# Mixture-of-experts layer: two experts in one float32 tile, experts sorted on chip, wider weight units

## The chip, the cores and the metric

The program runs on one core of a Trainium2 chip, in one launch. The metric is the device time of one execution in microseconds (us), lower is better; each figure for a kernel is the median of several executions. One further execution was recorded by the profiler, and every row shown below is from that one.

## The reference, cut to what matters

Two layers of a diffusion transformer work on 256 latent tokens (and, in the first layer, 256 context tokens) of width 1024. Everything up to the last stage is the same in both kernels. The last stage is a mixture of experts on the 256 latent tokens:

```python
logits = (t @ router)                          # [256, 8]
top_val, top_idx = lax.top_k(logits, 2)
gates = sum(one_hot(top_idx, 8) * softmax(top_val)[..., None], axis=1)
for e in range(8):
    he = silu(t @ w_gate[e]) * (t @ w_up[e])   # 1024 -> 3584
    out = out + gates[:, e:e+1] * (he @ w_down[e])   # 3584 -> 1024
```

All arrays are float32. An expert has three matrices of 1024 x 3584 (14.7 MB each), all eight 352 MB. Each token goes to two experts, so the experts get 64 tokens on average. For the inputs that the reference draws with its default seed the eight counts are 36, 68, 77, 79, 34, 67, 89 and 62.

## The kernel before, in words

An expert's tokens are gathered into 128 slots by a product with a selection matrix; the result is kept transposed (feature by slot) as the stationary operand of TensorE, and the weights stream through as the moving operand, 512 columns at a time. To keep float32 accuracy at the rate of the rounded type float32r, every operand is held in two parts, high and low, and each product is three matmuls (`mm3`: high x high, low x high, high x low). The tokens are split once; the weights are split as they come: ScalarE (ACT) writes the high part `wh`, VectorE (DVE) the low part `wl`, each 1024 columns at a time.

Weights come in units of 1 MB ([128, 2048] float32). All are loaded by the queue of SyncE (SP), in program order, into a ring of places: four named `w`, two `x1w`, two `mw`, two `zw`, that is ten; in the first round five more places that later hold something else are used as well (`gw`, two `yw`, two `sp`). A place is free again when VectorE has made the low part from it. A unit of the gate or up matrix is four blocks of 128 rows by 512 columns (2 KB runs in memory), one of the down matrix two blocks by 1024 columns (4 KB runs).

The eight experts go one after another, each in seven chunks of 512 hidden units. `up_chunk` does the gate and the up product of a chunk (4 units), then silu, product and transposition; `down_chunk` adds the chunk before it into two PSUM banks (2 units). So an expert takes 42 units and 504 matmuls of 512 columns, plus 28 transpositions. After an expert `finish` evacuates the result and `scatter` puts it back on token rows. The engines run in the order that a scheduler chose at build time; each engine and each queue is strictly in order.

If an expert has more than 128 tokens a slow second round runs (`overflow_expert`, behind a branch at the end); with the counts above it does not.

Of the kernel before, what the change touches and what calls it, by code (L numbers as in the profile page):

```python
# [28 lines left out]
def build(tc, A, out, stages=("s0", "mix0", "ffn0", "mix1", "moe"), dbg=None):  # L29
# [57 lines left out]
    # ---------------------------------------------------------------- constants  # L87
# [8 lines left out]
    # conditions and parameter rows -> columns  # L96
# [34 lines left out]
    # token tiles: 0, 1 = ctx; 2, 3 = x  # L131
# [48 lines left out]
    def sqrt_table(after):  # L180
        """the table of the square root, ahead of its use, once the column after is there"""
# [7 lines left out]
    def rsqrt_(ss, n, inv_n, name, bias=None):  # L189
        """1 / sqrt(ss * inv_n + bias), [P, n]: the square root of ScalarE and a Newton step; bias: eps"""  # L190
# [11 lines left out]
    # ---------------------------------------------------------------- ada  # L202
# [60 lines left out]
    # pre-norm of the residual and modulation, transposed and split  # L263
# [41 lines left out]
    def prenorm_all(mod, h2, tp, perm=False):  # L305
        """from the residual in DRAM"""
# [6 lines left out]
    def boundary(t, x_, b2, rowg, mod, h2, tp, perm=False, store=None):  # L313
        """end of a branch and start of the next for one token tile"""
# [7 lines left out]
    def token_major(hH, hL, W, c0, cb_=None, gets=None):  # L322
        """[128 tokens, 512 columns] products of the four token tiles"""
# [12 lines left out]
    # residual stream in DRAM between its uses (token tiles: 0, 1 = ctx; 2, 3 = x)  # L336
# [14 lines left out]
    def postnorm(x_, b2, rowg, tp, ss=None, tmt=None, out_=None, eng=None):  # L351
        """x_ += rowg * rms_norm(b2), b2: two [P, 512] PSUM banks or SBUF halves; ss: sums of squares so far"""
# [3 lines left out]
        for h in range(2):  # L356
            if ss[h] is None:
                ss[h] = sumsq(b2[h], tp, *(("mdL", 2) if out_ else ()))
# [19 lines left out]
    # S5 operands in DRAM: E [(j, k'), g, (re | im, d, n)], F [(d, n), g, (re | -im, i, k)],  # L378
    # T [(j, k'), i, g, k], powers A [(d, n), level, (re re | -im im) by (g, part)]
# [11 lines left out]
    def reduce_angle(a, n):  # L391
        """a -> a - 2 pi round(a / 2 pi), in place; n: scratch"""
# [6 lines left out]
    def s5_prep():  # L399
        with tc.tile_pool(name="s5c", bufs=1) as pc_, ExitStack() as es5:  # L400
            # powers for E and F: re, im, re + im
# [112 lines left out]
            for g8 in range(8):  # L514
# [7 lines left out]
                # C: re, im, re + im, re - im; B: re, im, re + im, im - re  # L522
# [71 lines left out]
            # lag 0: both directions and the skip  # L594
# [15 lines left out]
    # hidden units of the SwiGLU, [unit, tile, token]  # L610
# [17 lines left out]
    def ffn_first(h2, tp, tag):  # L628
        """the first two tiles of hidden units: the contexts first, while the latents are being normed"""
# [15 lines left out]
    # =============================================================== layer 0 mixer  # L645
    later.append(ada_pair(1, 0))
    if "mix0" in stages:
        es0, es1, esB = ExitStack(), ExitStack(), ExitStack()
        open_ps(esB, "psB", 6)
        if True:  # L650
            mk = open_pool(es0, "mk")
            # ---- filters; norm of the tokens
# [40 lines left out]
            # the filter network on both halves of the partitions alike  # L693
# [16 lines left out]
            # high parts over low parts along the contraction  # L710
# [26 lines left out]
            def filter_spec():  # L737
                """spectra of the filters"""
# [52 lines left out]
            # k, v, q, token-major; q / k norm and rope; q^T, k^T  # L791
# [118 lines left out]
            # ---- hyena long convolutions and attention  # L910
# [7 lines left out]
            def conv_spec(src, o):  # L918
                """spectral product of the [P, 2, 512] token-major src with filter o"""
# [40 lines left out]
            def attn(s, h):  # L960
                """head h (kv head h // 4) of stream s: transposed weights [key, key tile, query]"""
# [58 lines left out]
        # =========================================================== layer 0: out projection  # L1020
# [35 lines left out]
    # =============================================================== layer 0: SwiGLU  # L1056
# [109 lines left out]
    def route_setup(mp, tp, hf):  # L1166
        """tables of the dispatch"""
# [5 lines left out]
        R_["tie"] = tp.tile([P, NE, NE], F32, name="tie")  # L1173
# [28 lines left out]
        # rank (ties: the lower index first): the two first are taken  # L1202
# [18 lines left out]
    def route_rows(t, x_):  # L1221
        """normed rows of a token tile, split"""
# [6 lines left out]
    def route_slots(tp, e2):  # L1229
        """slots of two experts: [token, (expert, slot)]"""  # L1230
        Sel = tp.tile([P, 2, 2, P], F32R, tag="Sel", name="Sel", bufs=1)
        for t in range(2):
            for e in range(2):
                V.tensor_scalar(Sel[:, t, e, :], iota, R_["posm"][:, t, e2 * 2 + e:e2 * 2 + e + 1], None, OP.is_equal)
        return Sel

    def route_gates(tp, m2):
# [3 lines left out]
        v = [m2.tile([P, 2, 1], F32, tag="md%s" % "HL"[i], name="v%d" % i) for i in range(2)]  # L1241
# [13 lines left out]
        b = bank("cnt", "x")  # L1255
# [4 lines left out]
    def route_scatter(tp, Sel):  # L1260
        """the slots of two experts, transposed"""
        SelT = tp.tile([P, 2, 256], F32R, tag="SelT", name="SelT", bufs=1)
        b = bank("selT", "x")
# [5 lines left out]
        return SelT  # L1269

    def modulate(dst, src, k, vec):
        """one k tile of gathered normed tokens, modulated"""
# [10 lines left out]
    def moe_space():  # L1283
        """room on chip for the weights of the experts, as it comes free"""
        x1 = hp.tile([P, 2, 2048], F32, tag="hL", name="x1w")
        mw = moep.tile([P, 2, 2048], F32, name="mw")
        more_raw(x1[:, 0], x1[:, 1], mw[:, 0], mw[:, 1])

    def moe_first(sp, w0=()):
        """units of the first chunk ahead of the dispatch; the first round uses tiles needed later, too"""  # L1290
# [5 lines left out]
        ws = [kload(A["od_moe_w_gate"][0, 0], 4 * u, 0, 512) for u in range(2)]  # L1296

        def split():
            for u in range(2):
                first[0, u] = wsplit(ws[u], eng=G)  # L1300
        return split

    # =============================================================== layer 1 mixer
# [604 lines left out]
```

## Time and profile before

| | us |
|---|---|
| median of 3 runs (lowest, highest) | 2045.88 (2043.07, 2050.94) |
| profiled execution: span from first to last instruction | 2044.3 |
| of it from the first expert matmul to the last one | 1048.3 to 2027 |

The profiled execution has no time of its own beside its span; its span lies 1.6 us under the median. In the table of slices a digit is the busy share of a 51 us slice in tenths. `PEclk` in a window is the granted TensorE clock as a share of full speed (1.00 is 2.4 GHz, 0.50 is 1.2 GHz). DMA is the mean busy share of the core's 16 DMA engines; it can pass 1 because a packet's time overlaps the next one's.

### The profile page before, as it was taken

How to read it: one execution, taken by the hardware profiler on the slowest of the kernel's cores; microseconds unless marked ns; L12 is line 12 of the kernel's file. 1: busy time of each engine (PE TensorE's matmuls, PEld its weight loads, DVE VectorE, ACT ScalarE, POOL GpSimd, SP SyncE). 2: the span in 40 equal slices, each digit the busy share in tenths (PEclk: the TensorE clock that was granted, in tenths of full speed). 3: DMA queues.
4: the chain of work that ended last, by engine and by line, in shares of the span. 5: the costliest groups of instructions: out<-in, count | busy, mean ns of one | idle time of the engine just before them, and what ended most of it. 6: DMA issues, size and time to landing. Idle time of an engine off the chain costs nothing. (4 is left out here: it accounts for less than half of the span.)

```text
span 2044.3 us, 26454 instructions
## 1 busy us (share of the span) xinstructions
PE 1913.2 (94%) x9648; PEld 1502.6 (74%) x9648; DVE 1605.5 (79%) x2224; ACT 1210.1 (59%) x1679; POOL 160.6 (8%) x143
## 2 busy tenths in 40 slices
PE   5999999989999998965879999999999999999997
PEld 2667667867777786754768888888888888788885
DVE  6575775688775476487689999998899898998987
ACT  3532355543332365423668778777777777777775
POOL 1000310001011001045310000000000000000000
PEclk9999999999999999977979999999999999999998
DMA  9474315437657557627777999999999999999992
GB/s 342 163 253 154 131 42 177 157 108 229 209 196 230 206 202 264 228 82 267 280 265 277 384 354 345 339 367 378 344 352 357 368 369 338 342 383 366 361 373 94
DMA packets 246123, 545.59 MB, mean 267 GB/s; under 512 B 32619, under 2 KB 62420, under 8 KB 238436
## 3 DMA queue, kind: packets, MB, share of 16 engines
q1 hardware_dynamic: 215036, 514.73, 69.7%
q10 hardware_dynamic: 29400, 23.50, 3.9%
q0 software_dynamic: 1552, 5.62, 1.0%
q8 instruction: 78, 1.28, 0.3%
q14 instruction: 57, 0.47, 0.1%
HBM read 517.85 MB, written 25.89 MB: 266 GB/s over the span
## 5 line engine op out<-in xcount | busy, mean ns | idle before, releaser
L187 DVE TENSOR_TENSOR wl<-w,wh 128x1024 fp32r<-128x1024 f32 x396 | 471.5, 1225 | 103.6 <-ACT wh L186 97.3
L186 ACT ACTIVATE wh<-w 128x1024 fp32r<-128x1024 f32 x406 | 410.5, 1054 | 159.9 <-PE gu L178 52.4
L177 PE MATMUL yb<-wh,mdL 128*128 128x512 f32 x448 | 179.9, 402 | 0.0
L178 PE MATMUL mgu<-wl,xgH 128*128 128x512 f32 x448 | 176.1, 393 | 0.3
L176 PE MATMUL yb<-wh,mdH 128*128 128x512 f32 x448 | 176.3, 394 | 0.0
L178 PE MATMUL mgu<-wl,xB 128*128 128x512 f32 x448 | 175.7, 392 | 0.3
L177 PE MATMUL mgu<-wh,xgL 128*128 128x512 f32 x448 | 175.9, 393 | 0.0
L176 PE MATMUL mgu<-wh,xgH 128*128 128x512 f32 x448 | 175.9, 393 | 0.0
L177 PE MATMUL mgu<-wh,xB 128*128 128x512 f32 x448 | 174.9, 390 | 0.0
L176 PE MATMUL mgu<-wh,xB 128*128 128x512 f32 x448 | 174.6, 390 | 0.0
L187 DVE TENSOR_TENSOR wl<-zw,wh 128x1024 fp32r<-128x1024 f32 x132 | 155.5, 1219 | 15.0 <-ACT wh L186 13.0
L187 DVE TENSOR_TENSOR wl<-x1w,wh 128x1024 fp32r<-128x1024 f32 x132 | 156.4, 1219 | 11.8 <-ACT wh L186 9.1
L187 DVE TENSOR_TENSOR wl<-mw,wh 128x1024 fp32r<-128x1024 f32 x132 | 156.1, 1219 | 10.9 <-ACT wh L186 8.3
L178 PE MATMUL yb<-wl,mdH 128*128 128x512 f32 x448 | 151.4, 393 | 0.0
L176 PE MATMUL gu<-hH,wh 128*128 128x512 f32 (+1 forms) x384 | 145.9, 380 | 2.2 <-ACT hH L186 2.2
L178 PE MATMUL gu<-hL,wh 128*128 128x512 f32 (+1 forms) x384 | 144.3, 377 | 0.0
L177 PE MATMUL gu<-hH,wl 128*128 128x512 f32 (+1 forms) x384 | 143.4, 374 | 0.0
L186 ACT ACTIVATE wh<-x1w 128x1024 fp32r<-128x1024 f32 x134 | 135.6, 1054 | 11.2 <-PE mgu L177 7.3
L186 ACT ACTIVATE wh<-mw 128x1024 fp32r<-128x1024 f32 x132 | 133.8, 1054 | 11.2 <-PE mgu L177 7.6
L186 ACT ACTIVATE wh<-zw 128x1024 fp32r<-128x1024 f32 x132 | 133.2, 1053 | 10.0 <-PE mgu L177 5.9
L178 PEld LDWEIGHTS mgu<-wl,xB 128*128 128x128 f32 x448 | 84.0, 188 | 23.3 <-DVE wl L187 2.7
L178 PEld LDWEIGHTS mgu<-wl,xgH 128*128 128x128 f32 x448 | 84.2, 188 | 21.6 <-DVE wl L187 2.1
(668 smaller groups left out, 3845.3 us busy)
## 6 DMA issues: line engine op xcount, KB each, us to landing
w<-in_ada_w_dram SPq DMA_DIRECT2D x48, 1024.0 KB
w<-in_od_moe_w_up_dram SPq DMA_DIRECT2D x45, 1024.0 KB
w<-in_od_moe_w_down_dram SPq DMA_DIRECT2D x44, 1024.0 KB
w<-in_od_moe_w_gate_dram SPq DMA_DIRECT2D x43, 1024.0 KB
mw<-in_od_moe_w_gate_dram SPq DMA_DIRECT2D x23, 1024.0 KB
zw<-in_od_moe_w_up_dram SPq DMA_DIRECT2D x23, 1024.0 KB
x1w<-in_od_moe_w_down_dram SPq DMA_DIRECT2D x23, 1024.0 KB
w<-in_ev_ffn_w_down_dram SPq DMA_DIRECT2D x22, 1024.0 KB
```

The costliest lines, as they stand in the source:

```text
L176: T.matmul(b, aH, bH, start=start, stop=False)
L177: T.matmul(b, aL, bH, start=False, stop=False)
L178: T.matmul(b, aH, bL, start=False, stop=stop)
L186: S.activation(h, src, AF.Copy)
L187: (eng or V).tensor_tensor(l, src, h.bitcast(F32), op=OP.subtract)
```

## The change

- Experts 0 and 1 stay as they are. Experts 2 to 7 are sorted by their token count on chip (`route_order`): six register values then say which expert stands at which place, and the loads of places 2 to 7 take the expert's number from a register (`eload`).
- The four places 2 to 5 with the larger counts are done as before, with three matmuls per product. The last two places (the two smallest counts) share one tile: 64 slots each, one in the left half and one in the right half of TensorE's columns. Their products are plain float32 matmuls on the unsplit weights (`up_pair`, `down_pair`): one matmul per expert in place of three, two experts side by side.
- Chunks are 1024 hidden units wide (the fourth of an expert is 512), and a unit of gate or up weights is two row blocks by 1024 columns. In `up_big` the two column halves of a unit are done one after the other, each over both row blocks.
- The four chunks of the pair are put between those of the six other experts, at places 2, 8, 14 and 20 of the list of 28 tasks.
- The ring has eight places: the two `mw` are gone (their room goes to the pair's tiles). `mdH` and `mdL` have one buffer of twice the width in place of two.
- The second round starts at 64 tokens for the two experts of the pair, at 128 for the others.

The core of the diff (new functions whole, the rest cut):

```diff
+    def eload(W, e, k0, c0, n):
+
+        if isinstance(e, int):
+            return kload(W[e], k0, c0, n)
+        nk = 2048 // n
+        w = raw_tile()
+        SY.dma_start(w.rearrange("p (k c) -> p k c", k=nk),
+                     W[bass.ds(e, 1), k0 * P:(k0 + nk) * P, c0:c0 + n].rearrange("o (k p) c -> p (o k) c", p=P))
+        return w
...
+        return [nc.values_load(numi[0:1, i:i + 1], engines=[mybir.EngineType.SP], min_val=0, max_val=NE - 1)
+                for i in range(n)]
...
-        mw = moep.tile([P, 2, 2048], F32, name="mw")
-        more_raw(x1[:, 0], x1[:, 1], mw[:, 0], mw[:, 1])
+        more_raw(x1[:, 0], x1[:, 1])
...
+            def up_big(s, c, xH, xL, so):
+                o, w = piece(c)
+                nh, nk = w // 512, 2048 // w
                 bs = []
                 for i, W in enumerate((Wg, Wu)):
...
+                    bb = [bank("mgu", "gu", 4) for _ in range(nh)]
+                    for u in range(KD // nk):
+                        get = first.pop((s, c, i, u), None) or wsplit(eload(W, num[s], nk * u, o, w))
+                        for h in range(nh):
+                            for kk in range(nk):
+                                k = nk * u + kk
+                                mm3(bb[h], xH[:, k, so:so + P], xL[:, k, so:so + P],
+                                    *get(kk * w + h * 512, 512), k == 0, k == KD - 1)
+                    bs.append(bb)
+                return hidden(bs)
+
+            def up_pair(c, xP):
+                o, w = piece(c)
+                nh, nk = w // 512, 2048 // w
+                bs = []
+                for W in (Wg, Wu):
+                    bb = [bank("pgu", "gu", 4) for _ in range(nh)]
+                    for u in range(KD // nk):
+                        ws = [eload(W, num[PAIR + i], nk * u, o, w) for i in range(2)]
+                        for kk in range(nk):
+                            k = nk * u + kk
+                            for h in range(nh):
+                                for i in range(2):
+                                    r = slice(64 * i, 64 * i + 64)
+                                    T.matmul(bb[h][r], xP[:, k, r], ws[i][:, kk * w + h * 512:kk * w + h * 512 + 512],
+                                             start=(k == 0), stop=(k == KD - 1))
+                    bs.append(bb)
+                return hidden(bs)
...
+            def down_pair(c, hT, yP):
+                o, w = piece(c)
+                bb = [bank("py", "gu", 4) for _ in range(2)]
+                for u in range(w // 256):
+                    ws = [eload(Wd, num[PAIR + i], o // P + 2 * u, 0, 1024) for i in range(2)]
+                    for f2 in range(2):
+                        f = 2 * u + f2
+                        for h in range(2):
+                            for i in range(2):
+                                T.matmul(bb[h][64 * i:64 * i + 64], hT[:, f * P + 64 * i:f * P + 64 * i + 64],
+                                         ws[i][:, f2 * 1024 + h * 512:f2 * 1024 + (h + 1) * 512],
+                                         start=(f == 0), stop=(f == w // P - 1))
...
+            PAIR = NE - 2
+            num = [0, 1]
...
+            tasks = [(s, c) for s in range(PAIR) for c in range(NP)]
+            for c, i in zip(range(NP), (2, 8, 14, 20)):
+                tasks.insert(i, (PAIR, c))
```

On the queue of SyncE, 20 units into the experts (the chunks of experts 0 and 1 that come first), before: the queue goes on with the next loads of the ring, whose addresses are known.

```order
L153 DMA w<-in_od_moe_w_down_dram 128x2x1024 x2
L153 DMA w<-in_od_moe_w_gate_dram 128x4x512
L153 DMA zw<-in_od_moe_w_gate_dram 128x4x512
L153 DMA zw<-in_od_moe_w_up_dram 128x4x512
L153 DMA x1w<-in_od_moe_w_up_dram 128x4x512
```

The same place after the change; `onumi` holds the six expert numbers, and the lines shown are the last of six reads of it and the first loads of the pair.

```order
L1316 TENSOR_LOAD onumi
L1316 ISA x2
L163 ISA
L163 DMA zw<-in_od_moe_w_gate_dram 128x2x1024
L163 ISA
L163 DMA x1w<-in_od_moe_w_gate_dram 128x2x1024
L163 ISA
```

Six reads of the table now stand in the queue, and each load whose expert comes from a register has one more instruction ahead of it.

On TensorE, a piece of one expert's gate product before (`mgu` is the PSUM bank, `wh` and `wl` the split weights, `xgH` and `xgL` the split tokens): three matmuls for each block of weights.

```order
L176 MATMUL mgu_9088<-wh_9090,xgH_8799 128x512
L177 MATMUL mgu_9088<-wh_9090,xgL_8800 128x512
L178 MATMUL mgu_9088<-wl_9091,xgH_8799 128x512
L176 MATMUL mgu_9088<-wh_9094,xgH_8799 128x512
L177 MATMUL mgu_9088<-wh_9094,xgL_8800 128x512
```

Where the pair's first chunk begins after the change (`pgu` are its two banks, `xP` the tokens of both experts; `zw` and `x1w` are here the units of its two experts):

```order
L188 MATMUL yb_8869<-wl_9476,mdH_9034 128x512
L1857 MATMUL mht_9493<-cpk_76,hd_9398 128x128 x4
L1844 MATMUL pgu_9509<-zw_8607,xP_9172 64x512
L1844 MATMUL pgu_9509<-x1w_8441,xP_9172 64x512
L1844 MATMUL pgu_9510<-zw_8607,xP_9172 64x512
L1857 MATMUL mht_9500<-cpk_76,hd_9401 128x128 x4
L1844 MATMUL pgu_9510<-x1w_8441,xP_9172 64x512
```

The pair's matmuls read the units as they were loaded; the two experts alternate, each into its own 64 partitions of a bank, and TensorE now waits for the load itself and not for a split.

## Rows read from the trace of the kernel before

**Rows 1.** The page: span, busy time, and 40 slices of the span.
```profile
span 2044.3 us, 26454 instructions
PE 1913.2 (94%) x9648; PEld 1502.6 (74%) x9648; DVE 1605.5 (79%) x2224; ACT 1210.1 (59%) x1679; POOL 160.6 (8%) x143
...
DVE  6575775688775476487689999998899898998987
...
DMA  9474315437657557627777999999999999999992
```
**Rows 2.** Windows over the expert stage: from:to, us, busy per engine (instructions), PEclk, DMA, GB/s.
```profile
1048.00:2027.00 979.00, 978.35 (x4433) 799.28 (x4431) 891.61 (x877) 747.36 (x832) 1.82 (x1) 1.00 0.95 345
1100.00:2000.00 900.00, 899.35 (x4072) 734.84 (x4071) 820.24 (x794) 685.33 (x762) 0.00 (x0) 1.00 0.99 360
```
**Rows 3.** Waits, 1100 to 2000: us in total, times, longest.
```profile
PEld mgu L178 <- DVE wl L187: 4.8, 12, 0.6
```
**Rows 4.** Waits of SyncE's queue, 1100 to 2000.
```profile
SPq L153 <- DVE wl L187: 751.4, 304, 7.3
```
**Rows 5.** Timeline of PE in mid-stage: start us, us, what; the first and last of eleven.
```profile
1499.73 0.40 PE L176 MATMUL mgu<-wh,xB 128*128 128x512 f32 x1
...
1502.02 0.39 PE L177 MATMUL mgu<-wh,xB 128*128 128x512 f32 x1
```
**Rows 6.** Groups by form, 1100 to 2000: busy us, mean ns, idle before.
```profile
L187 DVE TENSOR_TENSOR wl<-w,wh 128x1024 fp32r<-128x1024 f32 x248 | 291.9, 1219 | 24.7 <-ACT wh L186 20.8
L186 ACT ACTIVATE wh<-w 128x1024 fp32r<-128x1024 f32 x248 | 248.2, 1053 | 19.5 <-PE mgu L177 11.2 <-PE yb L177 5.5 <-PE mgu L178 1.5
L1727 DVE TENSOR_TENSOR hd<-mgu,hd 128x512 f32<-128x512 f32 x52 | 35.9, 690 | 18.9 <-PE mgu L178 18.9
L1730 PE MATMUL mht<-cpk,hd 128*128 128x128 f32 x204 | 30.8, 273 | 0.0
```
**Rows 7.** Timeline of PE in layer 0, two stretches with unsplit float32 matmuls.
```profile
265.10 1.88 PE L969 MATMUL sc<-kz,qT 128*128 128x512 f32 x4
...
105.14 1.07 PE L227 MATMUL adp<-w,scol 128*32 128x512 f32 x8
106.14 0.50 PE L176 MATMUL tm<-wh,hH 128*128 128x512 f32 x1
```
**Rows 8.** Timeline of SyncE's queue: the first expert loads, those around 1050, the last.
```profile
993.88 0.50 SPq L153 DMA_DIRECT2D gw<-in_od_moe_w_gate_dram  x1
...
1042.51 0.46 SPq L153 DMA_DIRECT2D x1w<-in_od_moe_w_down_dram  x1
1054.35 0.37 SPq L153 DMA_DIRECT2D x1w<-in_od_moe_w_gate_dram  x1
```
**Rows 9.** Windows with the DMA engines full, columns as in rows 2.
```profile
10.00:20.00 10.00, 4.24 (x16) 1.10 (x19) 5.58 (x14) 2.42 (x3) 2.04 (x4) 1.00 1.02 414
1004.00:1014.00 10.00, 10.00 (x45) 8.27 (x45) 7.10 (x11) 7.17 (x12) 0.63 (x1) 1.00 1.05 398
1125.00:1150.00 25.00, 25.00 (x112) 20.31 (x111) 22.83 (x22) 19.52 (x22) 0.00 (x0) 1.00 1.04 391
1175.00:1200.00 25.00, 25.00 (x113) 20.18 (x112) 24.17 (x26) 19.19 (x21) 0.00 (x0) 1.00 0.87 314
```
**Rows 10.** Timeline of PE: first and last expert matmuls.
```profile
1048.32 0.40 PE L176 MATMUL mgu<-wh,xgH 128*128 128x512 f32 x1
...
2026.57 0.62 PE L178 MATMUL yb<-wl,mdH 128*128 128x512 f32 x2
```
**Rows 11.** The line that reads a register from the chip's memory: min/median/max ns.
```profile
L1805 SPq TENSOR_LOAD <-mxi x1: 485/485/485, 1997.9 to 1997.9; - x1
L1805 SPq FUSED_REGOPS  x1: 177/177/177, 1998.4 to 1998.4; - x1
```
**Rows 12.** Windows where PE was short of work, columns as in rows 2.
```profile
885.00:895.00 10.00, 5.67 (x33) 4.47 (x31) 9.52 (x29) 2.33 (x5) 4.75 (x4) 0.94 0.51 168
895.00:915.00 20.00, 7.47 (x38) 7.47 (x38) 15.49 (x28) 5.55 (x12) 4.01 (x2) 0.52 0.06 21
```

More of the change, by code (lines that the diff above doesn't have):

```diff
@@ L1295, in moe_first @@
         r += [lambda: z[:, 0], lambda: z[:, 1]]
-        ws = [kload(A["od_moe_w_gate"][0, 0], 4 * u, 0, 512) for u in range(2)]
+        ws = [kload(A["od_moe_w_gate"][0, 0], 2 * u, 0, 1024) for u in range(2)]
         def split():
             for u in range(2):
-                first[0, u] = wsplit(ws[u], eng=G)
+                first[0, 0, 0, u] = wsplit(ws[u], eng=G)
         return split
@@ new lines, in build, with piece, hidden @@
+            NP = 4
+            def piece(c):
+                return c * 1024, min(1024, FFE - c * 1024)
+            def hidden(bs):
+                hds_ = []
+                for g, u in zip(*bs):
+                    hd = hd_tile()
+                    S.activation(hd, g, AF.Silu)
+                    V.tensor_tensor(hd, u, hd, op=OP.mult)
+                    hds_.append(hd)
+                return hds_
+            def up_big(s, c, xH, xL, so):
+                o, w = piece(c)
+                nh, nk = w // 512, 2048 // w
@@ new lines, in turn @@
+            def turn(hds_, pair):
+                n = 512 * len(hds_)
+                dH = m2.tile([P, 1024], F32 if pair else F32R, tag="mdH", name="hTP" if pair else "mdH", bufs=1)
+                dL = None if pair else m2.tile([P, 1024], F32R, tag="mdL", name="mdL", bufs=1)
+                for j, hd in enumerate(hds_):
+                    b = bank("mht", "mt", 1)
+                    for f in range(4):
+                        T.transpose(b[:, f * P:(f + 1) * P], hd[:, f * P:(f + 1) * P], ident)
+                    cs = slice(j * 512, (j + 1) * 512)
+                    if pair:
+                        S.activation(dH[:, cs], b, AF.Copy)
+                    else:
+                        split_to(dH[:, cs], dL[:, cs], b)
@@ L1749, in scatter @@
+            def scatter(acc, s, yH, yL):
                 for t in range(2):
+                    sT = SelT[PAIR][:, t * P:(t + 1) * P] if s == PAIR else SelT[s // 2][:, s % 2, t * P:(t + 1) * P]
                     for h in range(2):
-                        b = bank("sct", "gu" if t and e == NE - 1 else "x")
+                        b = bank("sct", "gu", 4) if t and s == PAIR - 1 else fbank("sct")
                         cs = slice(h * 512, (h + 1) * 512)
-                        T.matmul(b, SelT[e // 2][:, e % 2, t * P:(t + 1) * P], yH[:, cs], start=True, stop=False)
@@ L1754, in scatter @@
-                        T.matmul(b, SelT[e // 2][:, e % 2, t * P:(t + 1) * P], yL[:, cs], start=False, stop=True)
-                        V.scalar_tensor_tensor(acc[:, t, cs], b, gate[:, t, e:e + 1], acc[:, t, cs],
-                                               OP.mult, OP.add)
-            def finish(e, yb):
+                        T.matmul(b, sT, yH[:, cs], start=True, stop=False)
+                        T.matmul(b, sT, yL[:, cs], start=False, stop=True)
+                        if s == PAIR:
+                            V.tensor_tensor(acc[:, t, cs], b, acc[:, t, cs], op=OP.add)
+                        else:
+                            V.scalar_tensor_tensor(acc[:, t, cs], b, gate_of(t, s), acc[:, t, cs], OP.mult, OP.add)
@@ new lines, in build @@
+            for c, i in zip(range(NP), (2, 8, 14, 20)):
+                tasks.insert(i, (PAIR, c))
+            tasks.append(None)
+            pend, done, yP = None, [], None
+            for i, task in enumerate(tasks):
+                hd_ = None
+                if task is not None:
+                    s, c = task
+                    if s == PAIR:
+                        hd_ = up_pair(c, xP)
+                    else:
+                        if c == 0:
+                            ybs[s] = [bank("yb", "yb") for _ in range(2)]
+                        hd_ = up_big(s, c, *xs_[s // 2], (s % 2) * P)
+                for d in done:
+                    scatter(acc, *d)
+                done = []
+                if pend is not None:
+                    (s1, c1), d1 = pend
+                    if s1 == PAIR:
+                        if c1 == 0:
+                            yP = m2.tile([P, D], F32, name="yP", bufs=1)
+                        down_pair(c1, d1[0], yP)
+                        if c1 == NP - 1:
+                            done.append(finish(PAIR, yP))
+                    else:
+                        down_big(s1, c1, *d1, ybs[s1])
+                        if c1 == NP - 1:
+                            done.append(finish(s1, ybs.pop(s1)))
+                pend = (task, turn(hd_, s == PAIR)) if task is not None else None
+                if i == 0:
@@ new lines, in build @@
+            mxo = mp.tile([1, NE], F32, name="mxo")
+            mxc = mp.tile([1, 1], F32, name="mxc")
+            mxi = mp.tile([1, 1], I32, name="mxi")
+            V.tensor_tensor(mxo, cnt[0:1, :], R_["cap"][0:1, :], op=OP.subtract)
+            V.tensor_reduce(mxc, mxo, axis=AX.X, op=OP.max)
+            V.tensor_scalar(mxc, mxc, 0.0, None, OP.max)
+            V.tensor_copy(mxi, mxc)
+            rv = nc.values_load(mxi[0:1, 0:1], min_val=0, max_val=2 * P)
+            dP = [tc.dram_tile([NE, P, 4], F32, name="dP%d" % r) for r in range(2)]
@@ L1809, in build @@
+            with tc.tile_pool(name="ovf", bufs=1) as op_:
+                with tc.If(rv > 0):
+                    for r in range(2):
                         pk = hq.tile([P, NE, 4], F32, tag="hL", name="pk")
[L1810 removed]
+                        V.tensor_tensor(pk[:, :, 0:2], posm.rearrange("p t e -> p e t"),
+                                        R_["cap"].unsqueeze(2).to_broadcast([P, NE, 2]), op=OP.subtract)
+                        if r:
+                            V.tensor_scalar(pk[:, :, 0:2], pk[:, :, 0:2], float(-P), None, OP.add)
```

203 lines of the change are left out of this document (118 added, 85 removed).

## The prediction

> **What bounds the kernel now.** I first read the page: TensorE (PE) is busy for 94% of the span, and in the second half VectorE and the DMA engines stand near full too [rows 1]. So three resources may be the limit, and the expert stage has to be read by itself. Over its 979 us PE is busy for 978.35 us at the full clock [rows 2]. Then the waits: from 1100 to 2000 the longest wait of PE's weight loads, for a low part from VectorE, comes to 4.8 us in all [rows 3], while SyncE's queue waits 751 us for VectorE to free a place [rows 4]. The loads wait for the engines, not the engines for the loads. And matmuls of 512 columns start every 0.229 us (ten intervals in 2.29 us) [rows 5]: 4032 of them are 923 of the 979 us, and transpositions, gathers and scatters fill the rest. The stage is bound by PE, with VectorE at 820 of 900 us and DMA at share 0.99 and 360 GB/s close behind [rows 2]. What the change saves on PE therefore counts only until the next limit.
>
> **What it takes from PE.** Two experts lose 2 x 504 matmuls, 231 us. For them come 168 sets (112 gate and up, 56 down) of two float32 matmuls, one per expert. Nothing in the trace has two column groups of 64, so I take the price from both sides. Four unsplit float32 matmuls with 512 columns on the whole array take 1.88 us with the drain of the last, some 0.43 each [rows 7]. Eight in four column groups of 32 run from 105.14 to 106.14, so four side by side cost 0.5 us with the drain shared [rows 7]. A set is 0.44 us if its halves run side by side and 0.87 us if not; the group row is the nearer, so 0.44: 74 us in all, 146 at the other end. The Trainium skill (FP8 and Floating Point Precision, TensorE Precision Notes) says that true float32 takes four passes through the array. By that page a set would be four times 0.229, 0.92 us, and the pair 154 us. The row shows about two times 0.229, so I go by the row. With the pair's own gather (32 small products, about 4 us) PE alone would need 979 - 231 + 74 + 4 = 826 us: a saving of 153 us, and a kernel at 1891, if PE stayed the limit.
>
> **What the queue can give.** It can't stay so. All 336 units of 1 MB still have to come, and 336 MB x 1.0486 in 826 us would be 427 GB/s. Stretches with the DMA engines full give 398 GB/s with 2 KB runs, 391 with both kinds of run while all engines are busy, and 414 with 8 KB runs in the first layer [rows 9]. Where the share is lower (0.87) the rate is too (314) [rows 9]: there the loads had no place to go. After the change gate and up come in 4 KB runs, except in the fourth chunks (32 units). I take 400 GB/s for 4 KB, 2.62 us a unit, and 391, 2.68 us, for those 32; the ends are 414 (2.53 us) and 380 (2.76 us; the 360 of the stage at share 0.99, brought to share 1.04). The Trainium skill (DMA: Bandwidth & Descriptors, Where 436 GB/s comes from) says that about 358 GB/s per core is what memory gives. That is the stage's own mean, and by it a unit would take 2.93 us. The 398 and 414 of rows 9 speak against that as a ceiling.
>
> **The sum.** PE starts the experts at 1048.3 [rows 10]. Two chunks of 1024 and one down product come ahead of the pair: 20 units of 12 matmuls, 55 us, with transpositions and the pair's gather some 5 us, small waits 3 us: 1112. The first loads go out from 994 as before; the queue then stands still for want of places until about 1054 [rows 8], which the change does not alter (13 first places instead of 15). At 1112 the 20 units have been used and the ring of eight is full, so 28 have landed and 308 are to come.
>
> From there the queue is the limit, because the pair's chunk eats its units faster than they come: two units (5.2 us) feed four sets (1.8 us). A whole chunk of the pair is 24 units, 63 us of loads, for 21 us of PE. In the chunks between, PE takes 12 x 12 x 0.229 and transpositions, about 34 us, against 31.4 us of loads; the ring gains 2.6 us per chunk, 11 to 13 us from pair to pair. That is under its 21 us, so it never fills and the queue does not stop. So: 276 x 2.62 + 32 x 2.68 = 809 us.
>
> Six register reads of 0.485 us stand once in the queue [rows 11]: 3 us, behind 20 loads, and the table is long made by then. The extra instruction per addressed load is like the register operation of 0.18 us [rows 11]; the queue has 2.6 us per load and issues one in 0.37 to 0.50 [rows 8], so nothing, with the price in the rivals if that is wrong.
>
> At the end PE is behind the queue by what the ring gained after the pair's last chunk, five chunks x 2.6 = 13 us, and by the last unit's split and 12 matmuls (1.05 + 2 x 1.22 + 2.8) [rows 6], 6 us: 19.
>
> Two losses I can only bound. When PE waits for loads its clock may fall: from 895 to 915, with PE busy for 7.5 of 20 us, the granted clock was 0.52 [rows 12]. The pair has eight such steps (four up, four down); if each leaves 10 us at half clock, that is 40 us, if the queue's lead covers it, nothing. And behind the pair's silu and product (0.69 us [rows 6]) the splits of the next unit wait in the same queues: up to 2 us a step, 16 in all. I take 18 for both, in the lower half, since PE time between the pairs costs only what the ring cannot hold.
>
> After the last expert matmul 17 us of scatter and norm remain, as now [rows 1, 10]. The sum: 1112 + 809 + 3 + 19 + 18 + 17 = **1978** for a span that is now 2044; the median of the runs lies 1.6 above the profile's, so **1980 us**, 3.2% under 2045.88.
>
> **Costed at nothing.** VectorE loses a quarter of its splits (2 x 42 x 2 x 1.22 = 205 us): no gain by itself, it was not the limit. A wide unit holds its first half until 9 of its 12 matmuls instead of 6; the split (1.05 + 1.22 us [rows 6]) then has 3.4 us instead of 4.1 until PE needs it, enough while VectorE is on time; if it is late by a whole chunk's other work (1.4 us), PE waits some 0.3 us, 7 us over the stage, within the 18. Sorting is some 30 small operations on VectorE under the first chunk, which PE covers. Single `mdH` and `mdL`: the next use is a whole up product later. The second round does not run: the smallest counts are 62 and 34, the largest 89.
>
> **The rivals.**
> (a) Loads as the new limit, as above: 1945 to 2005, by the unit's ends (308 x 0.09 = 28 us down, 308 x 0.14 = 43 us up) and the 18 (0 to 56). Chance 0.66.
> (b) PE slow in and after the pair: groups of 64 that do not run side by side (+72 us of PE, most of it hidden behind loads, 10 seen), or a clock at half for long stretches (40 instead of the part in the 18): 2005 to 2030. Rows 12 speak for the clock, the eight matmuls of rows 7 against the first. 0.15.
> (c) Loads much faster, 414 GB/s, and the two losses hidden: 1915 to 1945. Only 8 KB runs show it. 0.07.
> (d) 360 GB/s is the queue's ceiling, PE and queue having been limits together: 2.91 us a unit, 308 units 896 us, no lead at the end (6 instead of 19), clock and splits hidden: 1112 + 896 + 3 + 6 + 17 + 1.6 = 2036, no change that shows. For it: share 0.99; against it: 398 at 1004 and 391 at 1125 [rows 9], and the 751 us for which the queue had no place [rows 4]. 0.07.
> (e) Slower: an addressed load holds SyncE longer than its data takes. 252 of the 308 are addressed; from 0.3 us over the unit's 2.62 the gain is gone, at 0.45 the time is 1112 + 809 + 113 + 3 + 6 + 17 + 1.6 = 2062. No addressed load is in the trace; an issue of 0.37 and a register operation of 0.18 would have to become 3.1. 0.05.
>
> **How the numbers follow.** Half a per cent (10 us) is about what runs of this kernel tell from no change. The likeliest is (a), 1980. The range 1940 to 2030 holds (a), (b) and a little of (c), and leaves out (d), (e) and most of (c). Faster: (a), (b), (c), 0.88; same: (d), 0.07; slower: 0.05.
>
> **What would show it.** The last expert matmul near 1961; DMA share over 1.0 and 390 to 405 GB/s from 1112 on; PE idle before the pair's products, ended by DMA into `w`, `zw` or `x1w`, some 3.4 us per two units and 60 us in all; pairs of matmuls at L1844 some 0.44 us apart; dips of the clock there. I am wrong if PE stays without idle time, if SyncE's issues lie over 2.6 us apart with its queue waiting for nothing, or if the rate stays at 360 with the share at 1.

## The result: 26 us faster where 66 were forecast

| | before | after |
|---|---|---|
| median of the runs (lowest, highest), us | 2045.66 (2043.07, 2050.94) | 2019.68 (2018.54, 2022.01) |
| span of the profiled execution, us | 2044.3 | 2016.8 |

The ratio is 0.9877, with a 95% interval of 0.9860 to 0.9893. The forecast was 1980 us: the direction is right and the time lies in the range given, but the gain is 26 us instead of 66, so 40 us are to be explained.

The page of the kernel after, its lines that answer to [rows 1] (busy time, then slices of 50 us):

```profile
span 2016.8 us, 25616 instructions
PE 1860.4 (92%) x9278; PEld 1369.1 (68%) x9278; DVE 1394.2 (69%) x2054; ACT 1037.2 (51%) x1492; POOL 160.2 (8%) x144
...
DVE  6575775688875476486778358935883588578886
...
PEclk9999999989999999887979999999999999999998
DMA  9474314436666656637557999899999999999992
```

PE lost only 53 us of busy time (1913.2 to 1860.4), where the forecast took 153 away. VectorE lost its 211 us (forecast 205). The clock of TensorE did not fall in the expert stage: its digits stay at 9 up to the last slice.

Windows of the expert stage after (from:to, us, busy per engine with instructions, granted clock, DMA share, GB/s), to be held against [rows 2]:

```profile
1100.00:1970.00 870.00, 846.38 (x3693) 601.67 (x3692) 609.61 (x602) 513.68 (x574) 0.00 (x0) 1.00 0.97 373
1120.00:1240.00 120.00, 116.67 (x496) 76.24 (x493) 69.82 (x64) 64.59 (x72) 0.00 (x0) 0.99 1.03 411
1260.00:1340.00 80.00, 79.08 (x366) 58.52 (x366) 59.71 (x65) 47.45 (x56) 0.00 (x0) 1.00 0.87 324
1340.00:1460.00 120.00, 114.55 (x490) 75.55 (x487) 74.21 (x73) 63.99 (x71) 0.00 (x0) 1.00 1.03 412
1460.00:1540.00 80.00, 79.09 (x356) 59.09 (x356) 57.69 (x54) 47.49 (x51) 0.00 (x0) 1.00 0.97 357
1540.00:1640.00 100.00, 96.18 (x416) 62.26 (x413) 59.08 (x59) 49.92 (x58) 0.00 (x0) 1.00 1.03 414
1740.00:1820.00 80.00, 76.95 (x319) 48.90 (x316) 50.89 (x52) 42.29 (x48) 0.00 (x0) 1.00 0.94 367
1820.00:1980.00 160.00, 156.59 (x687) 125.56 (x686) 138.46 (x133) 116.25 (x125) 0.00 (x0) 1.00 0.93 342
```

This table is the main finding. The stage has no single limit. For 100 to 120 us from each of the first three chunks of the pair on, the DMA engines run at 411 to 414 GB/s and PE has gaps (116.67 of 120, 114.55 of 120). Then come 80 us in which PE is busy for 79 and the loads fall to 324 or 357 GB/s. The fourth chunk of the pair, half as wide, shows no such rate (367 GB/s from 1740 to 1820), and behind it come 160 us at 342. What is short changes with the place.

The trace also gives the filling of the ring: the units whose bytes have landed, less the units that PE's matmuls have used up by then. Before the change this is 9.4 to 11 of ten places for nearly all of 1100 to 1970. After it, it is about 8 (full) from 1250 to 1330 and falls to 3.6 at 1350, 8 from 1460 to 1520 and falls to 3.2 at 1550 (two of these are being read by the pair's products, and some have landed only in part), and 8 again from 1650 to 1740. The fourth chunk takes it down to 6.2 only, and from 1810 to the end of the loads it stays at 8 or a little over: there a load can start only when PE has let go of a place.

The first matmul of the pair and the last one of the experts, in the timeline of PE after (start, us, what):

```profile
1109.21 0.64 PE L1844 MATMUL pgu<-zw,xP 128*64 128x512 f32 x1
...
1996.77 0.40 PE L188 MATMUL yb<-wl,mdH 128*128 128x512 f32 x1
```

So the pair starts where the forecast put it (1112), and the last expert matmul stands at 1997, where 1961 was said: the loss lies between the two.

Waits of PE's weight loads after, 1100 to 1960 (us in all, times, longest), beside the 4.8 us of [rows 3]:

```profile
PEld yb L188 <- DVE wl L197: 16.2, 16, 1.2
PEld pgu L1844 <- DMA w<-in_od_moe_w_up_dram: 4.0, 6, 1.7
PEld pgu L1844 <- DMA zw<-in_od_moe_w_up_dram: 2.9, 2, 1.5
```

The forecast wanted 60 us of waits for loads ahead of the pair's products. They are 7. The largest wait that is put down to an engine is another: in the down products (`yb`) PE waits for low parts from VectorE. Four more, for parts of the gate and up weights and for what the transpositions read, are 4.7 to 6.2 us each.

And the waits of SyncE's queue after, 1100 to 1960, beside [rows 4]:

```profile
SPq L163 <- DVE wl L197: 418.2, 177, 5.7
SPq L153 <- DVE wl L197: 104.2, 40, 5.6
SPq L163 <- PE pgu L1844: 69.3, 29, 7.6
SPq L163 <- PE py L1887: 39.1, 14, 7.5
```

The queue still waits for places, now also for the pair's own products (`pgu`, `py`) to let go of theirs. The forecast had said that it "does not stop". But such waits alone don't tell whether the loads stop: from 1120 to 1240, at 411 GB/s, the queue waits for `wl` for 62 of the 120 us too. The rates and the filling of the ring tell it.

### The profile page after: what moved, and what is told of

The parts are those of the page before. It is cut to its first block, busy times and chain, and to the rows that moved or that the text cites. A ratio compares the mean times of both kernels' runs of the same rounds, so it can differ in the third digit from the quotient of the medians.

```text
span 2016.8 us, 25616 instructions
## 1 busy us (share of the span) xinstructions
PE 1860.4 (92%) x9278; PEld 1369.1 (68%) x9278; DVE 1394.2 (69%) x2054; ACT 1037.2 (51%) x1492; POOL 160.2 (8%) x144
## 5 line engine op out<-in xcount | busy, mean ns | idle before, releaser
L197 DVE TENSOR_TENSOR wl<-w,wh 128x1024 fp32r<-128x1024 f32 x380 | 449.7, 1224 | 101.7 <-ACT wh L196 98.9
L196 ACT ACTIVATE wh<-w 128x1024 fp32r<-128x1024 f32 x390 | 395.4, 1055 | 190.8 <-PE dn L187 49.0
L196 ACT ACTIVATE wh<-zw 128x1024 fp32r<-128x1024 f32 x122 | 124.3, 1057 | 53.5 <-DMA zw<-in_od_moe_w_down_dram 29.3
L186 PE MATMUL yb<-wh,mdH 128*128 128x512 f32 x336 | 133.5, 398 | 0.7 <-ACT mdH L196 0.7
L187 PE MATMUL yb<-wh,mdL 128*128 128x512 f32 x336 | 132.4, 394 | 0.0
L188 PE MATMUL yb<-wl,mdH 128*128 128x512 f32 x336 | 116.0, 400 | 11.6 <-DVE wl L197 11.6
L186 PEld LDWEIGHTS mgu<-wh,xgH 128*128 128x128 f32 x448 | 84.7, 189 | 20.0 <-ACT wh L196 1.0
L187 PEld LDWEIGHTS mgu<-wh,xgL 128*128 128x128 f32 x448 | 84.7, 189 | 18.9
L186 PE MATMUL mgu<-wh,xB 128*128 128x512 f32 x224 | 88.2, 394 | 2.0 <-ACT wh L196 2.0
L186 PEld LDWEIGHTS gu<-hH,wh 128*128 128x128 f32 x384 | 73.6, 192 | 20.2 <-issue 5.9
L187 PE MATMUL mgu<-wh,xB 128*128 128x512 f32 x224 | 87.1, 392 | 0.0
L188 PE MATMUL mgu<-wl,xB 128*128 128x512 f32 x224 | 82.7, 394 | 0.1
```

What stands on the lines that cost most here:

```text
L186: T.matmul(b, aH, bH, start=start, stop=False)
L187: T.matmul(b, aL, bH, start=False, stop=False)
L188: T.matmul(b, aH, bL, start=False, stop=stop)
L196: S.activation(h, src, AF.Copy)
L197: (eng or V).tensor_tensor(l, src, h.bitcast(F32), op=OP.subtract)
```

## What a set of the pair costs

The timeline of PE after, at the start of the third chunk of the pair. The two experts' units are here `zw` and `x1w`, each going to its half of the columns:

```profile
1526.68 0.64 PE L188 MATMUL yb<-wl,mdH 128*128 128x512 f32 x2
1527.24 0.64 PE L1844 MATMUL pgu<-zw,xP 128*64 128x512 f32 x1
1527.25 0.64 PE L1844 MATMUL pgu<-x1w,xP 128*64 128x512 f32 x1
1527.72 0.59 PE L1844 MATMUL pgu<-zw,xP 128*64 128x512 f32 x1
1527.73 0.59 PE L1844 MATMUL pgu<-x1w,xP 128*64 128x512 f32 x1
1528.15 0.59 PE L1844 MATMUL pgu<-zw,xP 128*64 128x512 f32 x1
1528.16 0.59 PE L1844 MATMUL pgu<-x1w,xP 128*64 128x512 f32 x1
```

The halves start 0.01 us apart, so they do run side by side, and after 0.43 us (0.48 the first time) the next two records follow. That looks like the 0.44 of the forecast, until the records are counted. All `pgu` matmuls after, grouped by the unit they read (records, then min/median/max ns, first and last start):

```profile
L1844 PE MATMUL pgu<-w,xP x224: 592/592/643, 1114.3 to 1756.0; 128*64 128x512 f32 x112
L1844 PE MATMUL pgu<-zw,xP x112: 592/592/643, 1109.2 to 1752.5; 128*64 128x512 f32 x112
L1844 PE MATMUL pgu<-x1w,xP x112: 592/592/643, 1109.2 to 1755.9; 128*64 128x512 f32 x112
```

These are 448 records. The program has 112 gate and up sets of two matmuls, 224. **A float32 matmul leaves two records**, each of which moves 512 columns in 0.43 us. So a set takes 0.86 us, with its halves side by side. In [rows 7] the "four matmuls" were two, and the eight in column groups of 32 were four, one in each group, which took 1.00 us side by side. The trace of the kernel before shows this too: for the 48 units of this line the program has 192 matmuls, and the trace has

```profile
L227 PE MATMUL adp<-w,scol x384: 592/617/1062, 15.7 to 829.4; 128*32 128x512 f32 x192
```

## The experiments

All ran beside the kernel before, which took 2044.21 us beside the first four, 2044.17 beside the next three and 2044.55 beside the last two. Theory 1 was that the forecast's price of a set was wrong and TensorE stayed the limit; in the last two runs it is that the ring runs full in one part and empty in another. The rivals differ from run to run. In some runs part of the work is left out, and their results serve for the time alone. Where a figure is said to be counted by starts, it is the time from the start of each matmul record of PE to the start of the next one, added up over the expert stage.

**Half of the columns.** Behind the first block of each product the pair's matmuls do 256 of 512 columns; the rest of the pair's result is left out.

```diff
+n = 256 if k else 512
-T.matmul(bb[h][r], xP[:, k, r], ws[i][:, kk * w + h * 512:kk * w + h * 512 + 512],
+T.matmul(bb[h][r, 0:n], xP[:, k, r], ws[i][:, kk * w + h * 512:kk * w + h * 512 + n],
```

(and the same in `down_pair`).

> Leaves out part of the pair's products: after the first block of each sum the pair's matmuls take 256 of the 512 columns; all loads, evacuations and waits stay. Theory 1 (TensorE is still the bound, because a set of two float32 matmuls takes 0.94 us and not 0.44): 146 of 168 sets fall to half, 69 us less on TensorE, so 1950 to 1985 us, the upper part if loads then become the limit. Rival (the loads, most of them now addressed by a register, set the pace): within 10 us of 2020.

Measured 1999.78 us (1998.88 to 2004.99), ratio 0.9788 [0.9772, 0.9805]: 20 us under the change. It lies between the two theories. 146 of the 168 sets lose 0.43 us each, 63 us, and a third of that shows. With the sets nearly at the price of the forecast the time is still 20 us above the forecast, so the price is only half of the miss. And now the waits for loads ahead of the pair's products appear that the forecast had named: 37 us of PE's weight loads (7 in the change), of which these two lines are 22.6:

```profile
PEld pgu L1845 <- DMA w<-in_od_moe_w_up_dram: 17.1, 10, 3.1
PEld py L1889 <- DMA w<-in_od_moe_w_down_dram: 5.5, 4, 2.0
```

The windows of this run show where the rest went:

```profile
1120.00:1400.00 280.00, 254.28 (x1176) 183.87 (x1176) 173.06 (x172) 147.54 (x167) 0.00 (x0) 0.99 0.99 389
1260.00:1340.00 80.00, 77.24 (x378) 58.30 (x376) 56.42 (x61) 46.77 (x55) 0.00 (x0) 1.00 0.89 334
```

PE is now idle for 26 of 280 us, and still the loads slow down ahead of the second pair chunk (334 GB/s at share 0.89).

**Constants in place of registers.** The expert numbers of the six places are written into the program; the sorting stays.

```diff
-return [nc.values_load(numi[0:1, i:i + 1], ...) for i in range(n)]
+return [6, 3, 2, 5, 7, 4]
```

> The expert numbers of places 2 to 7 are constants (6, 3, 2, 5, 7, 4, right for these inputs alone), so no register is read and no load is addressed by one; the sort itself stays. Theory 1: nothing changes, 2012 to 2026 us. Rival (addressed loads hold SyncE's queue): 30 us or more faster, below 1990.

Measured 2021.51 us (2021.29 to 2022.52), ratio 0.9887 [0.9870, 0.9903]. Six register reads and the addressed loads cost nothing; rival (e) is out.

**Wide chunks alone.** Eight single experts with three matmuls, in chunks of 1024, and no pair.

```diff
-PAIR = NE - 2
-num = [0, 1]
+PAIR = NE
+num = list(range(NE))
...
-for c, i in zip(range(NP), (2, 8, 14, 20)):
-    tasks.insert(i, (PAIR, c))
```

> The wide chunks alone: eight experts one after another, unsorted, three matmuls per product, no pair, ring of eight places. Theory 1 (TensorE bound; 44 us of new waits come mostly from the wide chunk and its single buffers, 6 us or so per expert): 2046 plus 25 to 55, so 2070 to 2100 us. Rival A (the waits come from the pair, which blocks the queues of VectorE and ScalarE): 2046 to 2055. Rival B (4 KB runs pay by themselves): 2030 or less.

Measured 2058.15 us (2057.58 to 2059.11), ratio 1.0066 [1.0049, 1.0083]. This is 14 us more than before, between the expectations of theory 1 and rival A. The ring of eight and the single `mdH` and `mdL` are in this run too, so the 14 us are the price of the wide chunk together with them. Its waits, 1100 to 2030, against the 4.8 us of [rows 3]:

```profile
PEld yb L188 <- DVE wl L197: 17.9, 16, 1.2
```

This is the same wait, 16 times up to 1.2 us, that the full change has (16.2 us). So it comes without the pair.

**The pair in narrow chunks.** The pair as changed, but chunks of 512 and gate and up units in 2 KB runs as before.

```diff
...
-NP = 4
+NP = 7
...
-return c * 1024, min(1024, FFE - c * 1024)
+return c * 512, 512
...
-for c, i in zip(range(NP), (2, 8, 14, 20)):
+for c, i in zip(range(NP), range(4, 49, 7)):
```

> The pair alone: sorted experts and the float32 pair, but all chunks 512 wide and gate and up loads in 2 KB runs as before; the pair's seven chunks stand between those of the others, one in seven. Theory 1 with waits from the wide chunks: 2046 - 69 + 10, so 1980 to 2000 us. If the waits come from the pair: 2012 to 2030. If loads are the bound (rival): slower than the changed kernel, over 2030.

Measured 2031.43 us (2029.59 to 2033.05), ratio 0.9933 [0.9916, 0.9949]: 12 us slower than the full change, on the rival's side. Windows of this run:

```profile
1120.00:1960.00 840.00, 816.50 (x3528) 572.62 (x3527) 590.69 (x575) 491.67 (x553) 0.00 (x0) 0.99 0.99 366
```

The DMA engines are at a mean share of 0.99 and move 366 GB/s, with PE idle for 23 us. That fits loads that bind nearly everywhere, though the share alone doesn't say so: before the change it was 0.99 as well, and PE hardly lacked work [rows 2]. The wide chunk costs alone and pays beside the pair. That it pays by its longer runs, which came at 411 GB/s, is likely but not shown: this run also deals the pair out in seven chunks instead of four.

**Half of the pair's loads.** The second expert reads the units of the first, so 42 loads of 1 MB are left out (294 of the 336 are in the trace); PE does all it did. The expectation says 84, which is the number of all the pair's units. At 2.55 us a unit the 42 are 107 us of loads, not over 200.

```diff
-ws = [eload(W, num[PAIR + i], nk * u, o, w) for i in range(2)]
+ws = [eload(W, num[PAIR], nk * u, o, w)] * 2
```

(and the same in `down_pair`).

> The second expert of the pair uses the units of the first: 84 units of 1 MB are left out (the other expert's weights are wrong then), TensorE's matmuls stay all there. Theory 1 (TensorE is the limit: its matmuls with the pair's sets at 0.94 us, 910 us, and some 40 us of its own pauses): 2005 to 2020, at most 15 under the full change, which waits on loads in few places. Rival (the loads set the stage's end): 84 units less at 2.6 to 2.8 us are over 200 us of loads, and the time falls by 30 us or more, under 1990.

Measured 1978.19 us (1977.14 to 1978.28), ratio 0.9673 [0.9656, 0.9689]: 41.5 us under the change, the rival's side. Theory 1 as it stood falls: the loads hold up the full change by 41.5 us, although the waits name DMA for 7. Counted by starts, 23 of the 41.5 us lie in the pair's own products and right behind them (172.7 us in the change, 149.7 here), about half of them within the products and half where PE goes on from them to another one. Nearly all the rest lies in the products, transpositions and scatters of the single experts. There the loads may act at second hand: a late unit makes a late split, and PE's wait is put down to VectorE. ScalarE's splits did wait less for loads of down units into `zw` (29.3 us in the change, 7.1 here), but this path was not tested by itself. This run's timeline also gives the price of a set without waits:

```profile
1502.88 1.51 PE L1844 MATMUL pgu<-zw,xP 128*64 128x512 f32 x6
...
1530.50 0.50 PE L186 MATMUL yb<-wh,mdH 128*128 128x512 f32 x1
```

The 32 sets of a whole chunk's gate and up take 27.62 us, 0.863 each. The wait for low parts in its down products is 7.5 us (16.2 in the full change):

```profile
PEld yb L188 <- DVE wl L197: 7.5, 9, 1.2
```

**Both halves.** The two edits together (half of the pair's columns and half of its loads are left out).

> Half of the pair's loads left out as in the run with half of the loads, and the pair's matmuls after the first block on 256 of 512 columns as in the run with half of the columns. Theory 1 (TensorE is the limit, and with half of the columns alone the loads took over, so that 20 us of 69 showed): now all 69 us show, 1945 to 1960. Rival (the 20 us were all there was to get, because the rest of the pair is not paid by columns, or the pauses of the wide chunks grow with every gain): 1985 to 2000, as with half of the columns alone.

Measured 1937.16 us (1935.59 to 1937.94), ratio 0.9469 [0.9453, 0.9485], some 8 us under the lower end of theory 1. Alone, the columns bring 20 and the loads 41.5; together 82.5, which is 21 more than their sum. That is what two limits in turn look like: with half of the loads out of the way the same columns are worth 41 us instead of 20. Theory 1 had all that was taken off show, and that is 63 us. Counted by starts, the pair's part falls by 59 us (149.7 to 90.7), and the products and transpositions of the single experts grow by 18; the wait for low parts in the down products is back at 15.7 us (7.5 with half of the loads alone).

**Late silu.** The full change, but silu and product of a chunk stand behind the split of the first down unit in the program (`then` calls `hidden`).

```diff
-return hidden(bs)
+return bs
...
 def down_big(s, c, dH, dL, yb, then):
...
+    if u == 0:
+        then()
```

> The whole change, but silu and product of a chunk are put behind the split of the first down unit in the program, so that VectorE makes that unit's low part before it waits for the last up product. Theory 1 (TensorE is the limit, and its waits for the low part at the head of each down product, some 1.1 us each and 20 in all, are on the path): 2000 to 2012. Rival (the loads set the end, the waits only fill with ring): within 4 us of the full change, 2016 to 2024; slower than that if the transposition then waits for the late product.

Measured 2012.85 us (2011.99 to 2013.98), ratio 0.9842 [0.9826, 0.9858]: 6.8 us under the full change, just above the range of theory 1, and the fastest kernel here that computes all of it. In the change, VectorE's queue at the head of a down product (timeline of DVE; the value in brackets is its idle time and what ended it):

```profile
1313.14 1.29 DVE L1811 TENSOR_TENSOR hd<-mgu,hd 128x512 f32<-128x512 f32 x2 [1.58 <-PE mgu L188]
1314.34 2.35 DVE L197 TENSOR_TENSOR wl<-x1w,wh 128x1024 fp32r<-128x1024 f32 x2
```

and PE beside it:

```profile
1314.09 0.60 PE L1857 MATMUL mht<-cpk,hd 128*128 128x128 f32 x4
1315.61 0.72 PE L188 MATMUL yb<-wl,mdH 128*128 128x512 f32 x2 [0.92 <-DVE wl L197]
```

VectorE idles for 1.58 us because the product `hd` waits for the last up matmul, and both products stand ahead of the low part `wl` that PE needs first. A wide chunk has two such products in a row. With the edit, the same place:

```profile
1313.50 0.69 DVE L1811 TENSOR_TENSOR hd<-mgu,hd 128x512 f32<-128x512 f32 x1 [1.35 <-PE mgu L188]
1314.11 2.35 DVE L197 TENSOR_TENSOR wl<-x1w,wh 128x1024 fp32r<-128x1024 f32 x2
1316.38 0.68 DVE L1811 TENSOR_TENSOR hd<-mgu,hd 128x512 f32<-128x512 f32 x1
```

and PE beside it:

```profile
1315.38 0.73 PE L188 MATMUL yb<-wl,mdH 128*128 128x512 f32 x2 [0.32 <-DVE wl L197]
```

The scheduler still put one product ahead of the low part; the second moved behind it, and PE's wait fell from 0.92 to 0.32 us.

**Half of the columns, late silu.** Both edits (half of the pair's columns left out).

> The pair's matmuls after the first block on 256 of 512 columns (the outputs' other halves are left out), and silu and product behind the split of the first down unit: the two earlier edits together. With half of the columns a set costs about what the forecast priced, so this kernel asks what else the forecast missed. Theory 1 (TensorE's waits for a late low part, and then the ring that is full in the wide chunks and empty after the pair): 1988 to 1996, some 4 to 10 under half of the columns alone. Rival (with the cheap sets the loads alone set the end, and the waits only filled the ring): 1998 to 2002, no change to half of the columns.

Measured 1994.06 us (1992.17 to 1996.60), ratio 0.9752 [0.9736, 0.9769]: 5.7 us under half of the columns alone, as theory 1 said. This run meets two of the forecast's premises, the price of a set and, in good part, low parts in time, and stands 14 us above it. Windows of it:

```profile
1120.00:1240.00 120.00, 108.18 (x487) 78.09 (x486) 71.02 (x66) 65.83 (x72) 0.00 (x0) 0.99 1.03 411
1240.00:1340.00 100.00, 97.31 (x469) 73.82 (x468) 75.52 (x81) 59.73 (x71) 0.00 (x0) 1.00 0.93 355
1120.00:1920.00 800.00, 760.73 (x3473) 573.74 (x3472) 581.95 (x570) 490.96 (x548) 0.00 (x0) 0.99 1.00 389
```

The loads can do 411 and do 389 over the stage: they still fall behind in the second half of each turn.

**The pair's down product later.** On top of late silu, the down product of a pair chunk comes two places later, from a tile of its own.

```diff
 if s1 == PAIR:
...
-    down_pair(c1, d1[0], yP)
...
+    held = (i + 2, c1, d1[0])
...
+if held is not None and held[0] == i:
+    c1 = held[1]
...
+    down_pair(c1, held[2], yP)
```

> The whole change with silu and product late, and in addition the pair's down product two chunks later than it was, in a tile of its own, so that its 8 units do not follow the 16 of gate and up after one chunk of another expert. Theory 1 (over a stretch from pair to pair TensorE and loads need about the same time, and what is lost is lost because the ring of eight runs empty in one part and full in the other): smaller swings fit into the ring, 1990 to 2007. Rival (the loads are the limit on the whole, wherever the pair's units stand): 2010 to 2016, as with late silu alone.

Measured 2020.93 us (2020.26 to 2022.30), ratio 0.9882 [0.9865, 0.9898]: 8 us slower than late silu alone. Both theories missed. The waits of SyncE's queue from 1195 to 1260, around the first such down product:

```profile
SPq L153 <- PE py L1890: 23.6, 8, 7.2
SPq L163 <- DVE wl L197: 19.1, 8, 4.5
```

The pair's down units hold their places in the ring until PE comes to them, and the loads behind them wait for these places: the queue stands for up to 7.2 us at a time. That is no loss of this run alone, though: over 1120 to 1960 such waits come to 60 us here and to 52 with late silu, and there they are up to 7.5 us long. The ring shows why the test did not do what it was meant to do: the gate and up units of a pair chunk alone take it down as far as before (3.0 at 1140, 3.1 at 1360, 2.9 at 1560); only the second dip became smaller. Counted by starts, the 8 us lie at the transpositions (31.4 us against 25.9) and in the scatters (17.9 against 14.3), and the pair's own part is 171.3 us against 173.1. Why they grew, and whether smaller swings of the ring would help, stays open. A larger ring was not tried either.

## Why the prediction was off

**The set's price, the step that failed first.** "A set is 0.44 us if its halves run side by side and 0.87 us if not" joined two questions that are not one. The halves run side by side (0.01 us apart), and a set is 0.86 all the same, because [rows 7] were read as one record per matmul. The pair is 168 x 0.863 = 145 us of PE, not 74, and PE alone would need 979 - 231 + 145 + 4 = 897 us instead of 826; the stage took 950 (1046.9 to 1997.2). The Trainium skill (FP8 and Floating Point Precision, TensorE Precision Notes) says four passes; that gave 0.92 a set, and the trace agrees within 7%. I had set it aside for a row that I misread. The step that hangs on it, waits for loads ahead of the pair's products, was right in kind for the price it assumed: the run with half of the columns has 37 us of them (60 forecast), the change 7. Worth in time: with nearly all of the excess taken off (63 of 71 us), 20 of the 40 us. That is the share when the price goes first; with half of the loads gone the same columns are worth 41, so the shares below hold in this order and are not a sum of separate causes.

**"It never fills and the queue does not stop", the second step.** It went wrong on three numbers. A whole pair chunk takes PE 48 x 0.863 = 41 us, not 21. Loads of 4 KB runs come at 411 to 414 GB/s, not 400: 2.55 us a unit, 61 us for the 24 units of such a chunk. So the ring has to cover 20 us there, not 42. And a single expert's whole chunk gains it more than 2.6 us: PE takes about 35 (12 units at the 357 GB/s that the loads keep while they wait for it), the loads need 12 x 2.55 = 31. Four or five chunks now gain about as much as a pair chunk uses up, so the ring of eight is full before the next pair chunk (324 and 357 GB/s in the windows) and nearly empty in it (3.2 to 3.6 units, PE with gaps at 411 to 414). It is full for about half of the time from 1110 to 1960, and what the loads lose there is not made up later. In the forecast the loads from 1112 on took 809 us without a stop. At 412 GB/s they could have taken 308 x 2.55 = 785; the windows of the change show 373 GB/s on the mean instead. That this is a cost, and not idle time of an engine that doesn't matter, is shown by the run with half of the loads (-41.5 us) and by the pair of halves that together bring 21 us more than apart. Worth: what is left of the 40 us, some 14, by the run with half of the columns and late silu. That the swing of the ring is the whole of these 14 is argued and not shown: the one run that was to make it smaller made it smaller in one of two dips and came out 8 us slower.

**The late low parts, costed within the 18.** The forecast gave 0.3 us per wide chunk, 7 us in all. The single wait is 0.9 to 1.2 us, because it lies at the head of the down product behind two silu products and not at the change of units. It is 16 us of waiting, and 6 to 7 us of time in two runs.

**What was right.** The start of the pair (1109 for 1112), VectorE's relief (211 for 205 us, and no gain by itself), the tail (2016.8 - 1997.2 = 20 us for 17), and addressed loads at nothing (2021.51 beside 2019.68). The clock, put at up to 40 us, cost next to nothing: 0.99 to 1.00 in each window above. Of the rivals, (b) had the outcome (2005 to 2030, by PE in the pair) for a reason half right: it called the 72 us "most of it hidden behind loads, 10 seen", and 20 were seen. The ends of (a), 1945 to 2005, were narrower than its own terms: the slow unit alone (43 us up) gives 2023. Against (d): the Trainium skill (DMA: Bandwidth & Descriptors, Where 436 GB/s comes from) puts a core's memory at about 358 GB/s, and here 411 to 414 held for 100 us and more at a time; 373 was only the mean over turns.

## What to carry to other kernels

Before a duration is divided by a count of records, count the instructions in the program: an operation that needs several passes can leave several records each. When a change brings two engines near their limit together, don't add the longer of the two totals: go along the program in pieces, and ask in each piece whether the buffer between them runs full or empty, because what is lost where one waits for the other need not be made up later. And don't take the waits that a profile names for a queue as what the queue costs; cut its work and measure: the loads were named for 7 us of PE's waits and held up 41.

## What the hardware showed that was not expected

- An unsplit float32 matmul leaves two records of 0.43 us for 512 columns each (448 records for 224 matmuls), 0.86 us in all. Two such matmuls in column halves of 64 start 0.01 us apart and take 0.863 us together (27.62 us for 32 sets).
- Loads of 1 MB in 4 KB runs, while all engines work: 411 to 414 GB/s for 100 to 120 us. With gate and up in 2 KB runs: 366 GB/s over 840 us, at a DMA share of 0.99.
- The granted clock stayed at 0.99 to 1.00 in all windows of the expert stage shown, even where PE was idle for 26 of 280 us.
- A load whose address comes from a register cost nothing that can be measured (2019.68 against 2021.51 us with constants).
